# Expert weights in 256-row tiles with two rows to a partition, and later modulation blocks, in a two-layer mixture-of-experts kernel

## The chip, the cores and the metric

The kernel runs on one core of a Trainium2 chip. The metric is the device time of one launch in microseconds (us); less is better. Engines are named as in the profile: PE (TensorE matmul), PEld (its weight load), DVE (VectorE), ACT (ScalarE), POOL (GpSimd), SP (SyncE, which here only issues DMAs). L12 is line 12 of the kernel.

## The reference

All values are float32. A first block has two layers on 512 tokens `x` and, in layer 0, 256 context tokens `xc` (in layer 1 these only serve as keys and values). A layer is a modulated norm, an input projection, four mixers (short convolution, conformer convolution, windowed attention, global attention), an output projection, and an expert stage:

```python
def layer(x, xc, mods, cmods, ...):
    sh1, sc1, g1, sh2, sc2, g2 = split(mods, 6)
    h = rms_norm(x, n1) * (1 + sc1) + sh1
    parts = split_proj(h @ w_in)
    x_new = x + g1 * (concat([ya, yb, yc, yd]) @ w_out)
    h2 = rms_norm(x_new, n2) * (1 + sc2) + sh2
    x_new = x_new + g2 * expert_choice_ffn(h2, router, w_gate, w_up, w_down)

def expert_choice_ffn(h, router, w_gate, w_up, w_down):
    cap = 2 * t // 16
    aff = softmax(h @ router)
    gates, idx = top_k(swapaxes(aff, 1, 2), cap)
    xs = h[idx]
    y = (silu(xs @ w_gate) * (xs @ w_up)) @ w_down * gates
    return zeros.at[idx].add(y)
```

The modulation is `mods = silu(c) @ ada_w[l] + ada_b[l]`, with `ada_w` of 2 x 1024 x 6144, and the same with `c_ctx` for the context. There are 16 experts a layer with three 1024 x 1024 matrices each; an expert takes 64 tokens of `x` and, in layer 0, 32 of `xc`. A second block (gated delta rule, dilated attention, convolutional feed-forward) follows.

## The kernel before, in words

**Entry (L204 to L274, L340 to L400).** SP issues the loads of small parameter rows (`row_load`, L223 to L231, into `rows`), the tokens (`xin`, L234, and `cin`, L265), and four modulation blocks of layer 0 (`ada_load`, L189 to L198, 2 MB each in four pieces). A block is 512 columns of `ada_w`; the norm before the first projection needs blocks 0 to 3. `ada_gen` (L309 to L332) turns one block into its part of `M[l]`: eight matmuls (L318), a copy, four transposes (L327), a sum. Blocks 0, 2, 1, 3 are done in this order, then `norm1_first` norms eight k tiles (128 of 1024 columns each; L396 to L398), and `dense` runs.

**`dense` (L421 to L484).** For each unit of 128 output columns it loads a 512 KB tile `raw`, splits it into a rounded part `wh` (ACT, L442) and the rest `wl` (POOL, L443), and makes three products a k tile (L473, L475). The two query units of an attention take 64 columns of each of two heads, so they are loaded by two DMAs of 64 columns (`colload2`, L493; for the first, L272), in rows of 256 bytes.

**Experts (`experts`, L1026 on).** The routing takes token sums and logits, writes the normed tokens to DRAM (`hd`, L1132), and finds each expert's tokens by eight rounds of maximum (L1145 to L1149). In layer 0, modulation blocks 8 to 11 of layer 1 are made meanwhile (`ga`, stepped at L1120 and L1150), and two accumulators `sumx` and `sumc` in DRAM are zeroed (L1138). An expert gathers its rows of `hd` (L1209), transposes them and applies shift and scale (`xpose`, L1213 to L1230), and then runs gate (`ax`), up (`ux`) and down (`yx`) products, in the order g(e), d(e-1), u(e). In layer 0 a second set (`ac`, `uc`, `yc`) is for the context rows. Each product has eight units, each of 128 rows of a weight (512 KB). The results of experts 0 to 13 are added to `sumx` and `sumc` in DRAM by POOL's DMA; near the end these are read back (`rb`, L1308), transposed and added (`sums_add`), and the last experts' results are added by a scatter with one-hot matmuls (`scatter_x`, `scatter_c`).

**What sets the order of the loads.** `wload` (L1043 to L1056) issues the units in program order, each into the next of a ring of slots: `rawA` (18 in layer 0, 20 in layer 1), `raw` (5) and `rawB` (2 and 8). A slot is free when its matmuls are done. On SP a scheduler sets the order of the instructions by its own estimates.

Of the kernel before, what the change touches and what calls it, by code (L numbers as in the profile page):

```python
# [134 lines left out]
def main_kernel(ctx, tc, I, out, stop=None, dbg=None, manual=False):  # L135
# [37 lines left out]
    dx = pool(ctx, "dx", space=DRAM).tile([128, 8 * 768], F32)  # L173
# [44 lines left out]
    rows = ent.tile([128, 4, 128], F32)  # L218
    xin = xip.tile([128, 4, 1024], F32)
    cin = xip.tile([128, 2, 1024], F32)  # L220
    ada0 = ent.tile([128, 4, 4, 1024], F32)
# [20 lines left out]
    x_load(1)  # L242
    row_load(G, 0, "qn", I["q_norm_g"], 2, dup=True)
    row_load(G, 0, "kn", I["k_norm_g"], 2, dup=True)
    row_load(G, 0, "cbb", I["conv_b_b"].rearrange("l (h p) -> (l h) p", p=128), 4)
    row_load(G, 0, "lng", I["conv_ln_g"].rearrange("l (h p) -> (l h) p", p=128), 4)
    row_load(G, 0, "lnb", I["conv_ln_b"].rearrange("l (h p) -> (l h) p", p=128), 4)
# [3 lines left out]
    x_load(2)  # L251
    SY.dma_start(sinkb, bass.AP(tensor=I["sink"].tensor, offset=I["sink"].offset, ap=[[0, 128], [1, 8]]))
    row_load(SY, 0, "fg", I["final_g"].rearrange("(k p) -> k p", p=128), 8)
    row_load(SY, 0, "ln1", I["ln1_2"].rearrange("l (k p) -> (l k) p", p=128), 8)
    x_load(3)
# [3 lines left out]
    ada_load(0, 0, ada0[:, 0], hfs=(0, 1))  # L259
    row_load(SY, 3, "cq", I["conv_qkv_2"].rearrange("l t (h p) -> (l t h) p", p=128), 48)  # L260
    row_load(SY, 3, "fc", I["ffn_conv_2"].rearrange("l t (h p) -> (l t h) p", p=128), 66)
    ada_load(0, 0, ada0[:, 0], hfs=(2, 3))
    ada_load(0, 2, ada0[:, 2])
    for t in range(2):
        SY.dma_start(cin[:, t, :], I["ctx"][0, t * 128:(t + 1) * 128, :])  # L265
    ada_load(0, 1, ada0[:, 1])
    pre0 = {}
    pre0[0] = raw_tile().rearrange("p (k c) -> p k c", k=8)
    SY.dma_start(pre0[0], I["w_in"][0, :, 1536:1664].rearrange("(k p) c -> p k c", p=128))
    pre0[1] = raw_tile().rearrange("p (k c) -> p k c", k=8)  # L270
    for h in range(2):
        SY.dma_start(pre0[1][:, :, 64 * h:64 * h + 64],  # L272
                     I["w_in"][0, :, 1280 + 128 * h:1344 + 128 * h].rearrange("(k p) c -> p k c", p=128))
    ada_load(0, 3, ada0[:, 3])  # L274
# [34 lines left out]
    def ada_gen(l, blocks, pl, psp):  # L309
        g, o, n = RO["adab"]  # L310
        for b in blocks:
# [8 lines left out]
            if 3 < b < 11 or (l == 1 and b != 7 and b < 11):  # L320
                ada_load(l, b + 1, hfs=range(4 if l == 1 and b > 7 else 3))
# [10 lines left out]
            yield  # L332

# [7 lines left out]
    if True:  # L341
        with ExitStack() as e0:
# [4 lines left out]
            def rows_to_cols(g, n):  # L347
                p = pse.tile([128, 512], F32, name="rc")
                T.transpose(p[:, :n], rows[0:n, g, :], ident[0:n, 0:n])
                V.tensor_copy(cols[:, g, 0:n], p[:, :n])  # L350
# [6 lines left out]
            for t in range(6):  # L357
# [16 lines left out]
                if t == 1:  # L374
                    rows_to_cols(1, RO["n", 1])
# [1604 lines left out]
```

## Time and profile before

| | |
|---|---|
| Time, median of 3 runs (range) | 2650.71 us (2647.95 to 2651.56) |
| Profiled execution: its own time, its span | 2657.17 us, 2655.0 us |
| Busy in the span: PE, PEld, DVE, ACT, POOL | 93%, 57%, 41%, 33%, 24% |
| Moved by DMA | 584.08 MB, mean 220 GB/s |
| Mean granted TensorE clock, share of full | 0.971 |

PE looks busy all over, but a busy share over the span hides the stages: the two expert stages (about 500 to 1057 us and 1389 to 1868 us) move most of the bytes at 380 to 409 GB/s, while the second block from about 1870 us on moves 32 to 130 GB/s. The four views used below are the windows (busy time of each engine, clock, DMA share and GB/s in a stretch), the chain (the work that ended last at each moment, followed back; in each row start, duration, engine or DMA, tile and line), the timeline of an engine, and the waits.

### The profile page before, as it was taken

What the parts mean: (1) busy time and instruction counts of PE and PEld (TensorE: products, weight loads), DVE (VectorE), ACT (ScalarE), POOL (GpSimd) and SP (SyncE); (2) the same over time, 40 slices, a digit from 0 to 9 for tenths busy, and PEclk for the clock granted to TensorE, in tenths of its full rate; (3) what the DMA queues carried; (4) which work ended last, traced back from release to release, by engine and by line L of the source; (5) the groups of instructions that cost most, each with busy time, mean ns of one, the idle gap of its engine ahead of it and who ended that gap; (6) DMA issues with size and microseconds to landing.
All of it is one profiled execution on the core that took longest, in us unless ns stands there. A gap on an engine that the chain in (4) does not pass through costs nothing.

```text
span 2655.0 us, 41308 instructions
## 1 busy us (share of the span) xinstructions
PE 2476.4 (93%) x16415; PEld 1500.4 (57%) x16415; DVE 1092.9 (41%) x2371; ACT 870.2 (33%) x1769; POOL 637.8 (24%) x552
## 2 busy tenths in 40 slices
PE   7999999699999999899979989898899999999998
PEld 4766777344444333577753322132577787888886
DVE  4488852311111113689641102021665555444411
ACT  4544362211111110464531111110562435443422
POOL 3533112011111100633220000000333233444443
PEclk8999999899999999799989999999899999999999
DMA  8454455999999998222179999999421102333332
GB/s 281 140 165 139 149 177 197 322 383 385 385 386 385 388 394 313 58 59 52 61 289 386 394 398 399 399 404 409 130 67 32 40 25 64 95 96 96 92 96 67
DMA packets 324758, 584.08 MB, mean 220 GB/s; under 512 B 36864, under 2 KB 190007, under 8 KB 323927
## 3 DMA queue, kind: packets, MB, share of 16 engines
q1 hardware_dynamic: 311943, 555.16, 57.7%
q0 software_dynamic: 12480, 26.23, 4.1%
q8 instruction: 129, 2.11, 0.3%
q14 instruction: 62, 0.51, 0.1%
q10 hardware_dynamic: 144, 0.08, 0.0%
HBM read 556.74 MB, written 18.87 MB: 217 GB/s over the span
## 4 chain that ended last, share of the span: by engine, by line
PE 62%; DMA 21%; DVE 9%; issue 3%; POOL 2%; ACT 1%; SPq 1%; ACTq 0%; DVEq 0%; POOLq 0%
PE px L473 21%; DMA rawA<-in_w_gate_dram 4%; DMA rawA<-in_w_down_dram 4%; PE ax L1243 3%; DMA rawA<-in_w_up_dram 3%; PE yx L1243 3%; PE ux L1243 3%; PE g L473 2%; PE s L553 2%; PE y L584 2%; PE px L475 2%; DMA rawB<-in_w_gate_dram 2%; PE pt L565 2%; PE ac L1248 2%; PE pt L473 2%
## 5 line engine op out<-in xcount | busy, mean ns | idle before, releaser
L443 POOL TENSOR_TENSOR wl<-raw,wh 128x512 fp32r<-128x512 f32 (+1 forms) x312 | 408.2, 1311 | 962.0 <-ACT wh L442 768.1
L442 ACT ACTIVATE wh<-raw 128x512 fp32r<-128x512 f32 (+1 forms) x312 | 193.6, 625 | 441.2 <-PE px L473 211.0
L473 PE MATMUL px<-hh,wh 128*128 128x512 f32 x768 | 315.7, 412 | 6.4 <-DVE xT L1401 1.8
L473 PE MATMUL px<-hh,wl 128*128 128x512 f32 x768 | 313.1, 408 | 6.6 <-POOL wl L443 6.6
L473 PE MATMUL px<-hl,wh 128*128 128x512 f32 x768 | 314.6, 410 | 3.8 <-DVE hl L1019 1.9
L1225 ACT ACTIVATE xt<-tr,mod,a 128x64 f32<-128x64 f32 x256 | 86.9, 405 | 295.5 <-PE tr L1221 285.1
L473 PEld LDWEIGHTS px<-hh,wh 128*128 128x128 f32 x768 | 148.7, 194 | 41.2 <-issue 6.1
L473 PEld LDWEIGHTS px<-hh,wl 128*128 128x128 f32 x768 | 148.8, 194 | 39.7 <-POOL wl L443 7.3
L473 PEld LDWEIGHTS px<-hl,wh 128*128 128x128 f32 x768 | 148.7, 194 | 37.5 <-issue 3.8
L1369 DVE SCALAR_TENSOR_TENSOR Yx<-yx,gcol,Yx 64x512 fp32r<-64x512 f32 x36 | 27.0, 750 | 268.7 <-ACT Yx L1368 268.7
L1209 POOL DMA_INDIRECT xg<-hd,gidx x32 | 29.7, 927 | 431.9 <-PE tr L1221 398.3
L785 DVE SCALAR_TENSOR_TENSOR yT<-ub,cols,yT 128x512 f32<-128x512 f32 (+1 forms) x180 | 126.5, 718 | 0.6
L1243 PE MATMUL ax<-rawA,xt 128*32 128x512 f32 x856 | 116.8, 597 | 2.2 <-DMA rawA<-in_w_gate_dram 2.1
L1273 ACT ACTIVATE sa<-ax 128x512 f32<-128x512 f32 x32 | 19.1, 597 | 290.9 <-PE ax L1243 183.1
L1300 POOL DMA_INDIRECT sumx<-ys,place x14 | 22.0, 1571 | 376.5 <-ACT ys L1347 376.5
L1243 PE MATMUL ux<-rawA,xt 128*32 128x512 f32 x800 | 106.1, 594 | 0.1
L1237 PE MATMUL ux<-rawA,xt 128*64 128x512 f32 x328 | 87.3, 611 | 8.1 <-DMA rawA<-in_w_up_dram 8.0
L1237 PE MATMUL yx<-rawA,hT 128*64 128x512 f32 x316 | 81.5, 621 | 11.0 <-DMA rawA<-in_w_down_dram 10.0
L565 PE MATMUL pt<-tab,P 128*128 128x128 f32 x448 | 82.2, 284 | 6.8 <-DVE PT L571 4.3
L1368 ACT ACTIVATE Yx<-yx,gcol 64x512 fp32r<-64x512 f32 x36 | 24.6, 682 | 190.7 <-PE yx L1237 138.4
L1228 DVE TENSOR_SCALAR xt<-tr,a,mod 128x32 f32<-128x32 f32 x128 | 39.0, 310 | 115.0 <-ACT xt L1225 114.5
L1237 PE MATMUL ax<-rawA,xt 128*64 128x512 f32 x316 | 77.7, 612 | 7.6 <-DMA rawA<-in_w_gate_dram 7.2
(593 smaller groups left out, 4895.0 us busy)
## 6 DMA issues: line engine op xcount, KB each, us to landing
rawA<-in_w_gate_dram SPq DMA_DIRECT2D x186, 512.0 KB, 10.4
rawA<-in_w_up_dram SPq DMA_DIRECT2D x182, 512.0 KB, 10.2
rawA<-in_w_down_dram SPq DMA_DIRECT2D x151, 512.0 KB, 10.4
raw<-in_ada_w_dram SPq DMA_DIRECT2D x80, 512.0 KB, 5.7
raw<-in_w_down_dram SPq DMA_DIRECT2D x74, 512.0 KB, 10.2
raw<-in_w_gate_dram SPq DMA_DIRECT2D x62, 512.0 KB, 8.1
raw<-in_w_in_dram SPq DMA_DIRECT2D x56, 512.0 KB, 3.9
raw<-in_w_up_dram SPq DMA_DIRECT2D x55, 512.0 KB, 10.2
```

Of the source, the lines that this page charges most:

```text
L442: A.activation(wh[:, :n], raw[i][:, a:a + n], AF.Copy)
L443: G.tensor_tensor(wl[:, :n], raw[i][:, a:a + n], wh[:, :n].bitcast(F32), op=OP.subtract)
L473: T.matmul(px, lhsT=w[:, k % 4, :], rhs=h[:, k0 + k, 0:512], start=st, stop=sp_)
L475: T.matmul(pc, lhsT=w[:, k % 4, :], rhs=h[:, k0 + k, 512:nt], start=st, stop=sp_)
L553: T.matmul(s[:, :w], lhsT=q, rhs=k, start=(a == 0), stop=(a == len(mm) - 1))
L565: T.transpose(pt[:, (t - a) * 128:(t - a + 1) * 128], P[:, t * 128:(t + 1) * 128], ident)
L584: T.matmul(y[64 * g:64 * g + 64, bi * 128:(bi + 1) * 128], lhsT=vs[g][t], rhs=PTs[i, g][t // 4][:, (t % 4) * 128:(t % 4 + 1) * 128], start ...
L785: V.scalar_tensor_tensor(acc[:, j, o:o + n], src, w, acc[:, j, o:o + n], op0=OP.mult, op1=OP.add)
L1225: A.activation(xt[:, kk, 0:64], p[:, k * NX:k * NX + 64], AF.Identity, bias=M[l][:, 24 + kk, 0:1], scale=a2[:, kk, 0:1])
L1237: T.matmul(px[64 * g:64 * g + 64, :], lhsT=lx(u), rhs=w[:, 512 * hf:512 * hf + 512], start=first, stop=last)
L1243: T.matmul(px[32 * g:32 * g + 32, :], lhsT=lx(u)[:, 32 * (g % 2):32 * (g % 2) + 32], rhs=w[:, 512 * hf:512 * hf + 512], start=first, stop= ...
L1248: T.matmul(pc[32 * g:32 * g + 32, :], lhsT=lc(u), rhs=w[:, 256 * q:256 * q + 256], start=first, stop=last)
```

## The change

1. Expert weights come in tiles of 256 rows, `[128, 2, 1024]`: partition p holds rows 2p and 2p+1, one run of 8 KB, by one load of 1 MB (9 slots of `rawA` and 1 of `rawB` in layer 0, 10 and 4 in layer 1; together with 2 pairs of `raw` 12 and 16 slots). The pairs of `raw` are two loads of 512 KB, each with runs of 4 KB. A load is issued at every second unit. The rows of a matrix are so taken in another order; `hd` is written with its columns in the matching order, shift and scale are permuted once (`shsc`), and activation and product write the hidden values in that order.
2. In the loop over the experts SP keeps the program's order.
3. Blocks 8 to 11 of layer 1's modulation are loaded behind all of layer 0's expert weights, into slots of `rawA`, and made between the steps of the last scatter.
4. At the entry, tokens and blocks 0 and 2 come first, then `cin`, the first unit, blocks 1 and 3, the two query units as one pair of 256-column loads (1 KB runs; also at the later query units), and then most of the small rows. The first norm is made in two halves, tiles 0 to 3 after blocks 0 and 2, tiles 4 to 7 after 1 and 3, with `dense` started between.
5. `sumx` and `sumc` are zeroed in the output projection's stage, and read back and added one expert sooner.

```diff
+    for t in range(1, 4):
+        x_load(t)
+    ada_load(0, 0, ada0[0])
+    ada_load(0, 2, ada0[2])
...
+    SY.dma_start(pre0[0], I["w_in"][0, :, 1536:1664].rearrange("(k p) c -> p k c", p=128))
+    ada_load(0, 1, ada0[1])
+    ada_load(0, 3, ada0[3])
+
+    def pair_load(src, c0):
+
+        ts = [raw_tile(), raw_tile()]
+        for i, t in enumerate(ts):
+            SY.dma_start(t.rearrange("p (k c) -> p k c", k=4),
+                         src[512 * i:512 * i + 512, c0:c0 + 256].rearrange("(k p) c -> p k c", p=128))
+        return ts
+
+    pre0[1] = pre0[2] = pair_load(I["w_in"][0], 1280)
...
+                    norm1_first(range(4), a1)
+                    gd = dense(units, hh, hl, dw, psp, pre=pre0, ahead=4)
+                    next(gd)
+                    drain(ada_gen(0, (1, 3), sqp, psp))
+                    norm1_first(range(4, 8), a1)
...
+                    G.memset(lg[:, 0:512], 0.0)
+                    for acc_, n in zip(accs, (8, 4)):
+                        SY.dma_start(acc_.rearrange("(p a) c -> p (a c)", p=128).rearrange("p (b c) -> p b c", c=512),
+                                     lg[:, None, 0:512].to_broadcast([128, n, 512]))
...
-            units = [(w, e, u) for w, e in seq for u in range(8)]
+            units = [(w, e, u) for w, e in seq for u in range(4)]
+            if has:
+
+                units += [("ada", b, u) for b in range(8, 12) for u in range(2)]
...
-            slots = ["A"] * nA + ["W"] * 5 + ["B"] * nB
+            slots = ["A"] * (nA // 2) + ["W"] * 2 + ["B"] * (nB // 2)
...
+                    src = W[w][l, e, 256 * u:256 * u + 256, :].rearrange("(p i) c -> p i c", i=2)
                     if k == "W":
-                        r = raw_tile()
-                    elif k == "A":
-                        r = rwpA.tile([128, 1024], F32, name="rawA", bufs=nA)
+                        r = [raw_tile(), raw_tile()]
+                        for j in range(2):
+                            SY.dma_start(r[j], src[:, j, :])
                     else:
-                        r = rwpB[0].tile([128, 1024], F32, name="rawB", bufs=nB)
-                    SY.dma_start(r, W[w][l, e, 128 * u:128 * u + 128, :])
-                    wt[w, e, u] = r
+                        if k == "A":
+                            t = rwpA.tile([128, 2, 1024], F32, name="rawA", bufs=nA // 2)
+                        else:
+                            t = rwpB[0].tile([128, 2, 1024], F32, name="rawB", bufs=nB // 2)
+                        SY.dma_start(t, src)
+                        r = [t[:, 0, :], t[:, 1, :]]
+                    for j in range(2):
+                        wt[w, e, 2 * u + j] = r[j]
...
-                    ga = ada_gen(1, range(8, 12), mp, Psum(ps, {"yx": 1}, {"misc": "yx"})) if has else iter(())
...
-                    for _ in steps(ga, 2):
-                        pass
-                    wload(6 if l else 0)
+                    wload(3 if l else 0)
...
-                        if i in (2, 4, 6):
-                            for _ in steps(ga, 2):
-                                pass
...
-                        wload(1)
+                        wload(u % 2)
...
                         if last and has:
+                            next(ga)
                             sq_add(sp, stA[:, 0:512], xT[:, m, :], 512, m == 0, eng=G)
...
+                with tc.manual_schedule(engines={mybir.EngineType.SP}):
+                    gather(0)
+                    gather(1)
+                    xpose(0)
...
+                            if has and e in (12, 14):
+                                for t in ((4, 5), range(4))[e // 2 - 6]:
+                                    sums_load(t)
```

The order of SP's loads at the entry, before (`ada_89` holds all four modulation blocks, in four calls of L196 in the order 0, 2, 1, 3; `raw` of L269 and L272 are the first two units):

```order
L196 DMA ada_89<-in_ada_w_dram 128x2x512 x6
L265 DMA cin<-in_ctx_dram 128x1024 x2
L196 DMA ada_89<-in_ada_w_dram 128x2x512 x4
L269 DMA raw<-in_w_in_dram 128x8x128
L272 DMA raw<-in_w_in_dram 128x8x64 x2
L196 DMA ada_89<-in_ada_w_dram 128x2x512 x4
L621 DMA dx<-xT 128x4096
```

and now (`ada_96`, `ada_97`, `ada_94`, `ada_95` are blocks 0, 2, 1, 3; L232 and L234 are the small rows):

```order
L239 DMA xin<-in_x_dram 128x1024 x3
L199 DMA ada_96<-in_ada_w_dram 128x2x512 x4
L199 DMA ada_97<-in_ada_w_dram 128x2x512 x4
L252 DMA cin<-in_ctx_dram 128x1024 x2
L254 DMA raw<-in_w_in_dram 128x8x128
L199 DMA ada_94<-in_ada_w_dram 128x2x512 x4
L199 DMA ada_95<-in_ada_w_dram 128x2x512 x4
L262 DMA raw<-in_w_in_dram 128x4x256 x2
L232 DMA raw<-in_q_norm_g_dram 2x64 x2
```

The last two blocks moved ahead of the query loads, and the small rows behind these.

PE in layer 0's routing, before, from the end of the top-k on (`tg` and `ti` are its results, `xg` the gathered rows of expert 0, L318 and L327 the modulation's matmuls and transposes):

```order
L1161 MATMUL tr<-tab,tg 128x80
L1162 MATMUL tr<-tab,ti 128x80
L318 MATMUL yx<-raw,s_74 32x512 x4
L1221 MATMUL tr<-tab,xg 128x96 x5
L318 MATMUL yx<-raw,s_74 32x512 x2
L1221 MATMUL tr<-tab,xg 128x96 x3
L1243 MATMUL ax<-rawA,xt 32x512 x4
L1248 MATMUL ac<-rawA,xt 32x256 x4
L1243 MATMUL ax<-rawA,xt 32x512
L318 MATMUL yx<-raw,s_74 32x512 x2
```

and now:

```order
L1205 MATMUL tr<-tab,tg 128x80
L1206 MATMUL tr<-tab,ti 128x80
L1265 MATMUL tr<-tab,xg 128x96 x8
L1287 MATMUL ax<-rawA,xt 32x512 x4
L1292 MATMUL ac<-rawA,xt 32x256 x4
```

No modulation matmul stands between the top-k and the experts any more. They stand on PE in the tail of layer 0 now, between the last `yc`, the scatter (L1448 for `x`, L1476 for the context) and layer 1's sums (L310):

```order
L1292 MATMUL yc<-rawB,hT 32x256 x4
L1367 MATMUL tr<-tab,rb 128x128 x4
L326 MATMUL ux<-rawA,s_76 32x512 x5
L1448 MATMUL tr<-oh,Yx 128x512
L326 MATMUL ux<-rawA,s_76 32x512 x3
L1448 MATMUL tr<-oh,Yx 128x512 x3
L335 MATMUL ux<-tab,ys 128x128 x4
L1448 MATMUL tr<-oh,Yx 128x512 x4
L326 MATMUL ux<-rawA,s_76 32x512 x6
```

The first block's matmuls moved ahead of the scatter's first; the other three follow among its later ones. On SP their loads stand behind the last weights and ahead of layer 1's first projection:

```order
L1092 DMA raw<-in_w_down_dram 128x1024 x4
L1098 DMA rawB<-in_w_down_dram 128x2048
L1081 DMA rawA<-in_ada_w_dram 128x2x512 x16
L500 DMA raw<-in_w_in_dram 128x8x128
L262 DMA raw<-in_w_in_dram 128x4x256 x2
```

They moved behind every expert load of layer 0.

## Rows read from the trace of the kernel before

**Rows 1.** Windows: us, busy (count) of PE PEld DVE ACT POOL, PEclk, DMA share, GB/s.

```profile
0.00:50.00 50.00, 33.25 (x140) 14.69 (x141) 13.32 (x42) 22.43 (x44) 8.63 (x15) 0.90 0.93 315
...
450.00:500.00 50.00, 30.11 (x180) 16.91 (x179) 25.11 (x107) 13.01 (x20) 4.52 (x28) 0.81 0.70 249
...
550.00:850.00 300.00, 300.00 (x3642) 124.40 (x3638) 45.15 (x118) 40.07 (x100) 37.66 (x28) 1.00 1.04 386
...
850.00:1050.00 200.00, 196.22 (x2220) 74.75 (x2210) 42.10 (x112) 28.65 (x68) 17.81 (x17) 1.00 1.02 380
...
1050.00:1100.00 50.00, 39.25 (x172) 24.81 (x173) 39.45 (x83) 25.02 (x47) 16.44 (x14) 0.73 0.12 38
...
1400.00:1850.00 450.00, 406.80 (x1730) 120.32 (x1726) 70.28 (x104) 67.36 (x165) 11.54 (x13) 1.00 1.03 399
...
1900.00:2655.00 755.00, 734.96 (x3740) 589.82 (x3738) 351.52 (x623) 314.90 (x551) 294.45 (x230) 1.00 0.24 70
```

**Rows 2.** Chain of waits, 0 to 110 us: start, us, what.

```profile
24.78 5.11 SPq L272
...
29.93 4.29 SPq L272
...
36.24 6.55 DMA ada<-in_ada_w_dram
...
49.39 0.55 DVE xin L397
...
63.97 1.11 POOL hl L398
```

**Rows 3.** Chain of waits, 430 to 530 us.

```profile
463.40 3.60 DMA raw<-in_ada_w_dram
...
480.82 15.39 DMA raw<-in_ada_w_dram
...
504.64 6.05 DMA raw<-in_ada_w_dram
...
520.29 0.43 PE ux L1243 x4
...
525.01 0.81 PE tr L1221 x8
```

**Rows 4.** Chain of waits, 1340 to 1400 us.

```profile
1380.17 0.49 DVE idx L1147 x2
...
1384.05 4.07 DMA xg<-hd,gidx
...
1389.46 8.34 PE ax L1237 x32
```

**Rows 5.** Timeline of PE, 700 to 716 us: start, us, instructions.

```profile
702.57 1.04 PE L1243 MATMUL ax<-rawA,xt 128*32 128x512 f32 x8
...
703.86 1.04 PE L1243 MATMUL ax<-rawA,xt 128*32 128x512 f32 x8
```

**Rows 6.** Chain of waits, 1000 to 1130 us.

```profile
1044.30 7.13 DMA rb<-sumx
...
1057.29 0.69 ACT Yx L1368
```

**Rows 7.** Timeline of PE, 451 to 530 and 1050 to 1100 us.

```profile
464.97 0.66 PE L327 MATMUL yx<-tab,sq 128*128 128x128 f32 x4 [0.74 <-ACT sq L323]
...
465.91 2.19 PE L318 MATMUL yx<-raw,s 128*32 128x512 f32 x8 [0.28 <-DVE mod L329]
...
1083.39 0.80 PE L473 MATMUL px<-hh,wh 128*128 128x512 f32 x1 [1.17 <-ACT hh L416]
```

**Rows 8.** Windows of layer 1's experts and of the load of xT.

```profile
379.00:380.00 1.00, 1.00 (x12) 1.00 (x10) 1.00 (x4) 0.81 (x2) 1.00 (x2) 1.00 1.02 418
...
380.00:381.00 1.00, 1.00 (x9) 0.80 (x8) 1.00 (x2) 0.00 (x0) 1.00 (x1) 1.00 0.95 393
...
1820.00:1840.00 20.00, 20.00 (x87) 6.91 (x83) 7.11 (x10) 0.60 (x1) 0.00 (x0) 1.00 1.03 410
```

More of the change, by code (lines that the diff above doesn't have):

```diff
@@ L332, in ada_gen, with rows_to_cols @@
             yield
+    def rows_to_cols(psp, name, g, n):
+        p = psp.tile([128, 512], F32, name=name)
+        T.transpose(p[:, :n], rows[0:n, g, :], ident[0:n, 0:n])
+        V.tensor_copy(cols[:, g, 0:n], p[:, :n])
     es_l0 = ExitStack()
@@ L379, in main_kernel, with norm1_first @@
             drain(ga)
-            for g in (0, 2, 3):
-                rows_to_cols(g, RO["n", g])
-            V.tensor_scalar(nsink, sinkb, -1.0, None, op0=OP.mult)
-        entry.close()
-        def norm1_first(sqp):
-            a1 = sqp.tile([128, 8, 2], F32, name="a1")
-            for k in range(8):
+        entry2.close()
+        def norm1_first(ks, a1):
+            for k in ks:
                 if k % 4 == 0:
@@ L429, in load @@
                     raw[i] = pre[i]
+                elif i < len(units) and len(units[i]) == 6 and units[i][5]:
+                    raw[i] = raw[i - 1]
+                elif i < len(units) and len(units[i]) == 6:
+                    raw[i] = units[i][0]()
                 elif i < len(units):
@@ L615, in layer @@
                 psp = Psum(ps, {"px": 3, "s": 2, "pt": 1, "misc": 1, "y": 1}, {"pc": "px"})
+                c0 = dict(a_b=0, a_c=256, a_h=512, b_v=768, b_g=1024, c_q=1280, c_k=1536, c_v=1664,
+                          d_q=1792, d_k=2048, d_v=2176)
+                evs = []
+                units = []
+                for n in "c_k c_q c_v b_g b_v d_k d_q d_v a_c a_h a_b".split():
+                    for j in range(2 if n[2] == "q" or n[0] in "ab" else 1):
+                        nt, ev = NT if n[2] == "q" or n[0] in "ab" else 768, partial(lambda i, px, pc: evs[i](px, pc), len(units))
+                        if n[2] == "q":
+                            units.append((partial(pair_load, w_in, c0[n]), ev, nt, 0, 8, j))
+                        else:
+                            units.append((colload(w_in, c0[n] + 128 * j), ev, nt))
                 if has:
                     hh, hl = hh0, hl0
-                    norm1_first(sqp)
+                    a1 = cst.tile([128, 8, 2], F32)
+                    norm1_first(range(4), a1)
[3 more added lines that the diff above has]
+                    norm1_first(range(4, 8), a1)
+                    entry.close()
                     xip_es.close()
@@ L938, in layer @@
                     ga = ada_rest()
-                gd = dense(u_c + u_b + u_d + u_a, hh, hl, dw, psp, pre=pre0 if has else {}, ahead=4 if has else None)
+                else:
+                    ga = iter(())
+                if not has:
+                    gd = dense(units, hh, hl, dw, psp)
                 at, cv = att_gen(), conv31()
                 w1, w2, w3 = (28, 28, 64) if has else (18, 18, 44)
-                run_all((dense_part(gd, 12), 12))
+                if has:
+                    for _ in range(2):
+                        next(gd)
+                    for g in (0, 2, 3):
+                        rows_to_cols(psp, "misc", g, RO["n", g])
+                    V.tensor_scalar(nsink, sinkb, -1.0, None, op0=OP.mult)
+                run_all((dense_part(gd, 9 if has else 12), 12))
                 run_all((dense_part(gd, 12), 12), (steps(at, w1), w1), (steps(ga, 8), 8))
@@ L1080, in experts @@
                 gidx = mp.tile([128, 16], I32)
+                shsc = mp.tile([128, 2, 8, 2], F32)
                 iota = mp.tile([128, 512], F32)
```

203 lines of the change are left out of this document (97 added, 106 removed).

## The prediction

> **What bounds the kernel now.** I read the table of windows first, to see which engine is full in which stage, then the chain of waits at each place where PE is not full. The reader should find four kinds of stage in [rows 1]. (a) The entry, 0 to 50 us: PE 33.25 of 50 us, DMA share 0.93 at 315 GB/s. (b) The routing of layer 0, 450 to 500: PE 30.11 of 50, clock 0.81. (c) The experts of layer 0, where both PE (300 of 300, then 196.22 of 200) and DMA (share 1.02 to 1.04, 380 to 386 GB/s) are full. (d) The experts of layer 1, 1400 to 1850: DMA share 1.03 at 399 GB/s with PE busy 406.80 of 450, so DMA sets the pace. The last 755 us are PE's (734.96 busy); the change does not touch them. All times below are from one execution of 2657.17 us (span 2655.0), 6.5 us above the median of 2650.71; I subtract the sum from the median.
>
> **A. Entry (+12 us).** In the chain, two q loads hold SP's queue for 5.11 and 4.29 us [rows 2]: 1024 rows of 256 B each. Behind them the last modulation block (in_ada) is issued and lands at 36.24 + 6.55 = 42.8. The norm begins at 49.4 and its eight k tiles end with hl at 65.1, 15.7 us or about 2 us a tile. The change puts the two q loads, as 256-column pieces with 1 KB rows, and all but four small row loads behind the blocks: block 3 then lands 9.4 us sooner, at about 33.4. Blocks 0 and 2 go first and let tiles 0 to 3 be normed before block 3 is there, so that only four tiles (7.9 us) remain after it. 33.4 + 6.6 (landing to first tile now) + 7.9 = 48, against 65.1: 17 us. The bounds are 5 (the dense steps that follow are held by POOL's and ACT's splitting of the weights, which does not get faster) and 17. I take 12, nearer the upper one, since the queue hold alone is 9.4. The remaining small loads then stand ahead of the next w_in load, some 18 issues on SP; the first three units are loaded by then, which covers them.
>
> **B. Routing of layer 0 (+23).** PE takes instructions in order, and modulation blocks 8 to 11 of layer 1 stand among the routing's. Three waits on their loads are on the chain: 3.60 us ahead of the top-k's input D, 15.39 after the top-k (where the transposes of the gathered rows stand behind), and 6.05 inside the first expert [rows 3]. The first up matmuls (ux) begin at 520.3. The top-k has ended where the second wait begins, 480.8; without the blocks it ends 3.6 sooner, at 477.2. Layer 1 shows the rest without such blocks: from the end of the last index (1380.7), over a gather of 4.07, to the first matmul (1389.5) it takes 8.8 us [rows 4]. So 486.0, plus eight units of 1.29 [rows 5] and one set of transposes (0.81, [rows 3]): ux at 497.1, 23 sooner. Bounds: 15, if the gather or the copies of ht are then late, and 25, the sum of the three waits. Added here are eight tiny matmuls and two DVE copies for the permuted shift and scale; they hide behind the top-k, which runs 12 us on DVE, and cost under 1 us if not. The zeroing of the accumulators (3 MB written, 8 us at 386 GB/s) goes ahead of the routing; behind it on SP stand weights first used after 486, which cover it.
>
> **C. Experts of layer 0 (+13).** From 550 to 850 PE gets 3642 instructions through in 300 us, 12.14 a us; from 850 to 1050 it is 2220 in 200, 11.10 a us [rows 1]. At the first rate those would take 183 us: 17 us are lost there, to weights that come too late once the lead of the first 25 tiles is eaten, and to the sums (rb waits 7.13 at the end, [rows 6]). After the change the lead at ux is larger (no block loads amid the weights) and rb is loaded one expert sooner. An expert is 24 units of 512 KB and two sets of transposes, 24 x 1.29 + 1.6 = 32.6 us on PE, 1.36 a unit. DMA brings 12.6 MB of weights and some 0.8 MB of gathered and added rows an expert (96 rows of 4 KB each way): 13.4 MB at 386 GB/s is 34.7 us, 1.44 a unit. With 8 KB runs in ten slots of twelve (E) I expect 1.41. Over the 15 experts that follow, that is a lag of 0.05 x 360 = 18 us, some 13 units: the lead at ux (24 loaded before the first expert, 8 used, some 5 brought back: about 21) lasts; at 1.44 it would be 29 us, 20 units, which leaves nothing for delays. Bounds 5 and 17; I take 13.
>
> **D. Tail of layer 0 (-7).** The blocks now come last in the weight stream and their matmuls stand between the scatter's on PE. One block is 2.19 us of matmuls and 0.66 of transposes [rows 7], four are 11.4. Between 1050 and 1100 PE is idle 10.8 of 50 us [rows 1]; I put 4.4 of the 11.4 into such gaps. Their 8 MB land about 22 us after the last weight at 386 GB/s, but that weight should land some 8 us ahead of PE's last use, and the last block is needed some 14 us after it: just in time. Bounds -2 (all hidden) and -15 (the loads late by 8). Layer 1's first w_in loads stand behind the blocks on SP; their tiles are first used at 1083.4 now [rows 7], 26 us after the last expert, and would land some 16 us after it (24 behind the last weight), so they are covered by about 10.
>
> **E. Experts of layer 1 (+10).** Here a faster load is a faster kernel. Weights in 4 KB runs alone make 410 GB/s at share 1.03; the one load with 8 KB runs in this trace, xT<-dx, makes 418 at share 1.02 in one full microsecond and 393 at 0.95 in the next [rows 8]. Brought to one share both are 3 to 4% more than 410; as they stand, 2% more and 4% less. 512 KB at 410 GB/s is 1.279 us; 3% is 0.038 a unit. 352 units are still to be loaded when this stage begins, 14 slots in 16 get long runs: 308 x 0.038 = 12 us. Against it, one slot less (1.3 us) and two units instead of one behind the last load (0.9). I take +10. Bounds: 393 GB/s gives 1.334 a unit, 308 x 0.055 = 17 us lost; 4% and no loss gives 16 won. The nearest row is the microsecond with the full share. [...]
>
> **F.** The second block's first weights are issued in program order instead of waiting for the last matmul: +1. ACT's and DVE's strided activation and product are used a pass later, ten us of cover.
>
> Sum: 12 + 23 + 13 - 7 + 10 + 1 = 52, so 2650.7 - 52 = **2598.7, say 2598.5 us**.
>
> **Rivals.** *Long runs are no faster* (chance 0.17): 8 KB behaves as 4 KB. For it: 393 in one of the two rows. Against: 418 in the other. E becomes -2 and C falls to 8, since the lead ends before the stream: 35 us, 2616. [...] *The blocks stall the tail* (0.12): the weights land no sooner than PE's last use, and PE waits behind 22 us of block loads with only 7 us of it covered, so D is -22: 2614. For it: DMA is full to the end of layer 0. *The entry's gain is not kept, or the change does not do what it says there* (0.10): the dense steps after it go by the splitting of weights, A is 5, or SP's order puts the row loads in the way: 2606. *Slower* (0.06): 8 KB runs are slower under load, for instance because gathered rows wait behind packets that are twice as long. With runs of 8 KB as fast as now the gain is the first rival's 35 us. Each 512 KB that takes d longer than 1.279 is lost 308 times in layer 1 and, the lead being gone, some 300 times in layer 0, so the point from which it decides is d = 35/608 = 0.058 us, 392 GB/s. At 10% less than 410, 369 GB/s (d = 0.142), it is 35 - 86 = -51: 2702. The 393 row is at this point, the 418 row speaks against it.
>
> **How the numbers follow.** My forecast has 0.55. The rivals but the last lie at 2606 to 2616. With the upper ends of A, B and E together it would be near 2580, and two of the milder rivals together near 2625: the range is 2578 to 2626, leaving about 0.1 above and 0.1 below. This kernel's measurement can tell about 0.2%, 5 us. Faster: 0.55 + 0.17 + 0.12 + 0.10 less a little for several mishaps at once, 0.91. Within 0.2%: 0.03, at 390 to 394 GB/s or with several losses at once. Slower: 0.06.
>
> **What would show it.** A: the first px at or before 45 and the last hl near 50, no wait of SP at the q loads. B: no PE wait on in_ada between 455 and 500 of the old scale, ux near 485 once A is taken off. C: PE's rate over 12 instructions a us until the last expert. D: the stretch from the last yc to the first px of layer 1 some 7 us longer than 26. E: 415 to 425 GB/s in stretches of layer 1 without gathers. I am wrong if these stretches show 410 or less, if PE waits on in_ada after the last expert for over 10 us, or if what the entry gains is gone by 100 us.

## The result, and the profile after

The changed kernel takes 2616.74 us (median of 4 runs, 2612.24 to 2619.82), the kernel before, on the same chips, 2651.14 (2647.95 to 2656.49). The ratio is 0.9867 with a 95% interval of 0.9844 to 0.9890: 34 us faster, where 52 were forecast (2598.5); the time lies inside the range that was given, near the first two rivals' 2614 to 2616. The profiled execution of the changed kernel took 2619.82 us, its span is 2618.1; against the profile of before that is 36.9 us of span.

Where these came from is read by cutting both spans at the same events of the trace: the copy of layer 0's logits (`lg`), the first up matmul (`ux`), the last down matmul (`yx`), layer 1's first projection matmul (`px`), its logits, its first gate matmul (`ax`), its last `yx`.

| Stage, us | before | after | gained | forecast |
|---|---|---|---|---|
| start to layer 0's logits | 458.2 | 448.9 | 9.3 | A 12 |
| to the first ux | 60.6 | 43.3 | 17.3 | B 23 |
| to the last yx of layer 0 | 538.4 | 530.7 | 7.7 | C 13 |
| to layer 1's first px | 26.2 | 31.5 | -5.3 | D -7 |
| to layer 1's logits | 279.1 | 275.7 | 3.4 | 0 |
| to its first ax | 27.0 | 28.2 | -1.2 | 0 |
| to its last yx | 478.7 | 473.6 | 5.1 | E 10 |
| the rest | 786.8 | 786.2 | 0.6 | F 1 |

The windows of the changed kernel (columns as in [rows 1]):

```profile
0.00:50.00 50.00, 35.77 (x178) 20.08 (x179) 21.74 (x54) 29.33 (x56) 11.79 (x14) 0.97 0.86 296
450.00:500.00 50.00, 35.97 (x321) 19.48 (x325) 25.95 (x112) 16.84 (x33) 3.71 (x4) 0.80 0.55 208
550.00:850.00 300.00, 300.00 (x3642) 124.46 (x3638) 44.58 (x117) 39.25 (x99) 36.59 (x27) 1.00 1.03 391
850.00:1000.00 150.00, 146.19 (x1695) 59.64 (x1691) 32.33 (x89) 23.73 (x56) 14.23 (x13) 1.00 1.02 400
1400.00:1800.00 400.00, 347.77 (x1516) 114.33 (x1516) 65.17 (x97) 58.38 (x143) 9.77 (x11) 0.99 1.02 406
1760.00:1810.00 50.00, 43.62 (x192) 14.15 (x189) 9.81 (x14) 5.03 (x12) 0.00 (x0) 1.00 1.01 418
```

Against [rows 1] and [rows 8] the reader sees the rate of DMA in layer 1's experts go from 399 to 406 GB/s, without gathers from 410 to 418, and in layer 0's from 386 to 391; PE still falls from 3642 instructions in 300 us to 1695 in 150, 11.3 a us, in the late experts of layer 0. The chain at the entry:

```profile
38.67 0.50 PE px L486
...
47.33 0.55 DVE xin L401
...
51.93 1.14 POOL hl L402
```

The tiles that came from 49.39 to 63.97 in [rows 2] have matmuls behind them from 38.67 on, and the last but one hl begins at 51.93. The chain in layer 0's routing:

```profile
448.93 0.69 DVE lg L999
...
468.94 0.49 DVE idx L1194 x2
...
473.46 4.29 DMA xg<-hd,gidx
...
479.40 1.87 PE ax L1287 x8
...
482.12 1.71 PE ax L1287 x8
...
484.61 0.86 PE ax L1287 x8
...
492.35 0.86 PE ux L1287 x8
```

Against [rows 3] no modulation load is left between the logits and ux. The gather is followed at once by the first gate matmuls, whose first two units take 1.87 and 1.71 us against 0.86 for the third: PE has just waited 7.3 us for the gather, and the granted clock is 0.50 until 484.4 and 1.00 from 484.6 on:

```profile
479.00:483.80 4.80, 4.80 (x31) 1.50 (x33) 2.44 (x8) 2.75 (x8) 0.90 (x1) 0.50 0.32 85
484.60:492.30 7.70, 7.70 (x103) 2.91 (x96) 0.00 (x0) 0.27 (x1) 0.00 (x0) 1.00 0.85 322
```

In the tail the blocks' matmuls (L326) stand among the scatter's (timeline of PE):

```profile
1023.81 1.91 PE L326 MATMUL ux<-rawA,s 128*32 128x512 f32 x10
...
1054.41 0.80 PE L486 MATMUL px<-hh,wh 128*128 128x512 f32 x1 [1.17 <-ACT hh L420]
```

and at the end of layer 1's experts (chain) the last load, now of 1 MB, is followed by two units of PE:

```profile
1814.81 15.09 DMA rawB<-in_w_down_dram
...
1829.94 1.96 PE yx L1281 x8
```

### The profile page after: what moved, and what is told of

It is laid out like the page before. It is cut to its first block, busy times and chain, and to the rows that moved or that the text cites. A ratio compares the mean times of both kernels' runs of the same rounds, so it can differ in the third digit from the quotient of the medians.

```text
span 2618.1 us, 40657 instructions
## 1 busy us (share of the span) xinstructions
PE 2440.2 (93%) x16447; PEld 1505.9 (58%) x16447; DVE 1096.5 (42%) x2375; ACT 869.1 (33%) x1769; POOL 630.8 (24%) x545
## 4 chain that ended last, share of the span: by engine, by line
PE 63%; DMA 22%; DVE 9%; POOL 2%; issue 2%; ACT 2%; SPq 0%; ACTq 0%; DVEq 0%; POOLq 0%
PE px L486 21%; DMA rawA<-in_w_down_dram 7%; DMA rawA<-in_w_gate_dram 4%; DMA rawA<-in_w_up_dram 3%; PE yx L1287 3%; PE ax L1287 3%; PE ux L1287 3%; PE g L486 2%; PE y L591 2%; PE s L560 2%; PE px L488 2%; PE pt L572 2%; PE pt L486 2%; PE s L486 2%; PE yc L1292 2%
## 5 line engine op out<-in xcount | busy, mean ns | idle before, releaser
L1269 ACT ACTIVATE xt<-tr,shsc 128x64 f32<-128x64 f32 x256 | 86.2, 405 | 280.8 <-PE tr L1265 273.8
L1287 PE MATMUL ux<-rawA,xt 128*32 128x512 f32 x1024 | 133.9, 594 | 0.0
L1287 PE MATMUL yx<-rawA,hT 128*32 128x512 f32 x976 | 127.6, 594 | 4.2 <-DMA rawA<-in_w_down_dram 3.6
L1281 PE MATMUL yx<-rawA,hT 128*64 128x512 f32 x288 | 70.7, 625 | 21.2 <-DMA rawA<-in_w_down_dram 21.2
L1272 DVE TENSOR_SCALAR xt<-tr,shsc 128x32 f32<-128x32 f32 x128 | 38.9, 310 | 117.8 <-ACT xt L1269 117.1
L1281 PE MATMUL ux<-rawA,xt 128*64 128x512 f32 x320 | 78.9, 601 | 9.2 <-DMA rawA<-in_w_up_dram 9.2
L1281 PE MATMUL ax<-rawA,xt 128*64 128x512 f32 x352 | 83.5, 609 | 1.9 <-DMA rawA<-in_w_gate_dram 1.8
```

The source lines that it names most:

```text
L1269: A.activation(xt[:, kk, 0:64], p[:, k * NX:k * NX + 64], AF.Identity, bias=shsc[:, 0, kk, 0:1], scale=shsc[:, 1, kk, 0:1])
L1281: T.matmul(px[64 * g:64 * g + 64, :], lhsT=lx(u), rhs=w[:, 512 * hf:512 * hf + 512], start=first, stop=last)
L1287: T.matmul(px[32 * g:32 * g + 32, :], lhsT=lx(u)[:, 32 * (g % 2):32 * (g % 2) + 32], rhs=w[:, 512 * hf:512 * hf + 512], start=first, stop= ...
```

## The experiments

Each is one edit to the changed kernel unless it says otherwise. Times are medians, ratios to the kernel before on the same chip, with 95% intervals; stage times are read as in the table above, from one profiled execution each.

**1. Short runs again.** Every 1 MB load becomes two of 512 KB with runs of 4 KB.

```diff
-                        SY.dma_start(t, src)
+                        for j in range(2):
+                            SY.dma_start(t[:, j, :], src[:, j, :])
```

> The changed kernel with each 1 MB weight load cut into two loads of 512 KB, one for each row of a partition, so that every run is 4 KB again; slots, order and all else stay. Theory (the length of the run is what the two expert stages gained by): layer 1's experts, from first gate matmul to last down matmul, go from 473.6 us back to about 479 to 481, stretches without gathers from 419 GB/s to 410, and layer 0's experts end 3 to 6 us later; in all 8 to 12 us slower than the changed kernel, about 2627. Rival (order and size of the loads, not the run): layer 1's experts stay at 473 to 475 and the time within 3 us of 2617.

Measured: 2633.23 us, ratio 0.9912 (0.9889 to 0.9934): slower than the changed kernel by 12 us going by the ratios, 16 by the medians. Layer 1's experts take 480.6 us (473.6 with long runs), layer 0's 538.6 (530.7). The windows:

```profile
550.00:850.00 300.00, 299.26 (x3630) 123.76 (x3622) 44.66 (x117) 39.33 (x99) 36.63 (x27) 1.00 1.03 385
850.00:1000.00 150.00, 144.56 (x1620) 55.16 (x1616) 29.84 (x83) 21.28 (x52) 14.24 (x13) 1.00 1.03 391
1400.00:1800.00 400.00, 357.80 (x1500) 103.44 (x1497) 60.82 (x90) 60.19 (x149) 10.37 (x12) 1.00 1.03 399
1760.00:1810.00 50.00, 45.98 (x194) 13.35 (x192) 11.13 (x16) 5.91 (x13) 0.00 (x0) 1.00 1.03 409
```

The rates are within 1% of those of before, 385, 391, 399 and 409 GB/s against 386, 387 (from 850 to 1000), 399 and 410, where long runs make 391, 400, 406, 418. The run length is worth 7.9 us in layer 0 and 7.0 in layer 1. The theory holds, a little above its upper bound in layer 0; and without long runs the paired tiles are 2 us behind the kernel before in layer 1 (480.6 against 478.7), which the forecast had as 2.2.

**2. Long runs, half the partitions a load.** To tell the run from the size of a load.

```diff
-                        SY.dma_start(t, src)
+                        for j in range(2):
+                            SY.dma_start(t[64 * j:64 * j + 64], src[64 * j:64 * j + 64])
```

> The changed kernel with each 1 MB load cut into two loads of 512 KB by partitions (0 to 63, 64 to 127), so that runs stay 8 KB and loads are as small as before. Theory (run length): as the changed kernel, layer 1's experts 473 to 475 us, about 2617, or up to 3 us better in layer 0, since a unit is held up by 512 KB and not by 1 MB. Rival (the size of a load): layer 1's experts near 479, about 2625.

Measured: 3279.68 us, ratio 1.2333 (1.2274 to 1.2393). Neither held; the windows in layer 1's experts say why:

```profile
1800.00:1850.00 50.00, 33.06 (x104) 9.95 (x104) 2.88 (x4) 4.44 (x11) 0.89 (x1) 0.75 1.02 233
1950.00:2000.00 50.00, 29.90 (x98) 8.65 (x100) 2.88 (x4) 4.44 (x11) 0.89 (x1) 0.79 1.02 227
```

DMA is busy all the time (share 1.02) and moves 227 to 233 GB/s: little over half of the changed kernel's 406 to 418 in this stage, at the same share (1.01 to 1.02). Runs are as long as there and loads as small as before, where the stage made 399 to 410; what neither kernel has is a load that covers 64 partitions in a row.

**3. Long runs, every second partition a load.** The same sizes and the same runs, but each load covers every second one of the 128 partitions.

```diff
-                        SY.dma_start(t, src)
+                        for j in range(2):
+                            SY.dma_start(t[j::2], src[j::2])
```

> The changed kernel with each 1 MB load cut into two of 512 KB by even and odd partitions, runs of 8 KB. With the lower and upper 64 partitions DMA fell to about 230 GB/s. Theory (half of the partitions in a row share half of the way into SBUF, and every second one does not): over 400 GB/s again, layer 1's experts 473 to 480 us, about 2617 to 2622; then run length alone, at the old load size, carries the gain. Rival (a load that covers 64 partitions is slow whichever they are): about 230 GB/s and 3250 us again.

Measured: 2643.82 us, ratio 0.9949 (0.9929 to 0.9969); layer 1's experts 475.9 us, layer 0's 548.6. The windows:

```profile
550.00:850.00 300.00, 290.83 (x3526) 121.46 (x3522) 44.63 (x117) 39.31 (x99) 36.64 (x27) 1.00 1.03 389
850.00:1000.00 150.00, 136.89 (x1603) 57.60 (x1596) 28.80 (x82) 18.58 (x44) 13.81 (x13) 0.97 1.00 386
1400.00:1800.00 400.00, 347.81 (x1542) 121.47 (x1538) 59.60 (x88) 61.10 (x152) 10.65 (x12) 0.97 1.02 405
1760.00:1810.00 50.00, 44.31 (x188) 14.47 (x184) 6.54 (x9) 8.12 (x20) 0.00 (x0) 0.91 1.01 418
```

The rate is back at 405 and 418 GB/s, as the theory had it, so what slowed experiment 2 was which partitions a load covers (of the way into SBUF the runs show these rates alone), and in layer 1 a load of 512 KB with long runs is within 2.3 us of one of 1 MB: there the run's length carries the gain. In layer 0 the time was missed: from 550 to 850 PE already loses (3526 instructions against 3642) at 389 GB/s, where the changed kernel has 391. The weights are not the reason. The waits of PE over this run's layer 0 experts (485 to 1034; us in total, times, longest) hold none for a weight:

```profile
PE tr L1368 <- DMA rb<-sumx: 7.2, 1, 7.2
PE tr L1266 <- DVE hT L1342: 6.8, 12, 0.6
PE tr L1341 <- DVE sa L1334: 6.7, 15, 0.5
```

In the changed kernel PE has no such wait before 850. Its transposes of `sa` stand among the gate units there, and those of the gathered rows among the up units. Here the scheduler has put both between the up units and the next gate units, where they wait for DVE, 13.5 us in all; a sum (`rb`) costs 7.2 more. It is 33.87 us from one expert's first gate matmul to the next's, 32.85 in the changed kernel. So in layer 0 the edit also changed PE's order, and the run says nothing there on the size of a load.

**4. The kernel before without blocks 8 to 11.**

```diff
-                    ga = ada_gen(1, range(8, 12), mp, Psum(ps, {"yx": 1}, {"misc": "yx"})) if has else iter(())
+                    ga = iter(())
...
-            if has:
-                ada_load(1, 8)
...
+    V.memset(M[1][:, 32:48, :], 0.0)
```

> The kernel before without modulation blocks 8 to 11 of layer 1: their loads and matmuls are left out and that part of the modulation is zero, so 8 MB and 11 us of PE are gone. Theory (the blocks' loads held layer 0's routing): the first up matmuls of layer 0 begin 18 to 24 us sooner than 518.8, at 495 to 501, and the experts end 18 to 28 sooner; about 2625 to 2632. Rival (the first expert was waiting for its weights or for the gather anyway): under 10 us, 2642 or more.

Measured: 2630.26 us, ratio 0.9911 (0.9894 to 0.9927). From the logits to ux it takes 43.8 us (60.6 before, 43.3 after): the waits were the blocks' and nothing else's. The first ux comes 24.8 us sooner (494.1 against 518.8), but 7.9 of them lie ahead of the logits (450.3 against 458.2), a stretch that varies by as much (last section). Its timeline of PE, two gate units and the first of ux:

```profile
482.46 1.94 PE L1242 MATMUL ax<-rawA,xt 128*32 128x512 f32 x8
...
485.02 1.04 PE L1242 MATMUL ax<-rawA,xt 128*32 128x512 f32 x8
...
494.06 1.03 PE L1242 MATMUL ux<-rawA,xt 128*32 128x512 f32 x8
```

Layer 0's experts then take 531.6 us, with 4 KB runs and single tiles: 6.8 less than in the kernel before, since the blocks' loads no longer stand amid the weights, and nearly the changed kernel's 530.7. These 6.8 and the 16.8 up to ux make the whole 24 us of the ratio. Beside experiment 1 (538.6, 4 KB runs, paired tiles, SP in program order) this puts the price of pairing, one slot of 25 less and a slot pair that frees only after two units, at some 7 us in layer 0: the long runs first had to pay for it. This is read from two runs; pairing alone was not undone, and program order may be up to 2 of the 7 (experiment 11).

**5. The changed kernel without blocks 8 to 11.**

```diff
-                units += [("ada", b, u) for b in range(8, 12) for u in range(2)]
+                pass
...
-                    ga = ada_gen(1, range(8, 12), Psum(sp, {"ys": None}, {"sq": "ys"}), Psum(ps, {"ux": 1}, {"misc": "ux"}))
+                    ga = iter(range(99))
...
+    V.memset(M[1][:, 32:48, :], 0.0)
```

> The changed kernel without modulation blocks 8 to 11 of layer 1: their loads and matmuls are left out and that part of the modulation is zero. Theory (in the tail the blocks cost PE time between the scatter's matmuls, 5 to 6 us): from the last yc matmul of layer 0 to the first px of layer 1 it takes 25 to 27 us instead of 31, about 2611. Rival 1 (they are hidden): within 2 us of 2617. Rival 2 (their 8 MB also hold back the rows read back for the sums or layer 1's first weights): over 9 us, 2607 or less.

Measured: 2610.82 us, ratio 0.9830 (0.9813 to 0.9846); the tail takes 26.1 us, layer 0's experts 531.5.

Its timeline of PE, from the last transpose of the sums to layer 1's first px:

```profile
1024.74 0.66 PE L1368 MATMUL tr<-tab,rb 128*128 128x128 f32 x4
...
1031.72 4.60 PE L1449 MATMUL tr<-oh,Yx 128*128 128x512 f32 x8 [0.49 <-DVE xT L1452]
...
1050.53 0.79 PE L487 MATMUL px<-hh,wh 128*128 128x512 f32 x1 [1.17 <-ACT hh L421]
```

The theory holds: 5.4 us in the tail (31.5 against 26.1) and nothing in the stage ahead of it, so the 8 MB behind the weights hold back nothing there. PE is the price, not the loads. The whole is 10 us by the ratios, of which the stages show these 5.4 alone; the two intervals touch, so the whole cannot tell 5 from 10. The windows of the two tails, first the changed kernel's, show why 80 matmuls more cost only this:

```profile
1023.00:1054.00 31.00, 26.59 (x142) 11.84 (x134) 22.15 (x49) 17.07 (x33) 15.22 (x13) 0.95 0.53 170
```

```profile
1024.80:1050.50 25.70, 17.38 (x56) 11.29 (x54) 19.81 (x42) 15.03 (x30) 12.77 (x11) 0.62 0.05 13
```

PE is 9.2 us longer busy and 3.9 less idle, and with the blocks among the scatter's matmuls the granted clock is 0.95 instead of 0.62; the scatter's own 32 matmuls take 9.7 us in all instead of 12.8 (sums over the timelines). In the tails of nine kernels with the blocks there (the changed one, experiments 1, 3 and 7 to 12) it is 0.94 to 0.99, in four without (the kernel before, experiments 4, 5 and 6) 0.56 to 0.73.

**6. The blocks in layer 1's body.** Loaded and made there between its projection and attention steps; their loads and steps in layer 0's tail are left out as in experiment 5.

```diff
-                    ga = iter(())
+                    ga = ada_gen(1, range(8, 12), sqp, psp)
```

> The changed kernel with modulation blocks 8 to 11 of layer 1 made among layer 1's projection and attention steps, where DMA has a share of 0.23, instead of in layer 0's tail. The tail is 5.4 us shorter without them. Theory 1 (PE has gaps in layer 1's body which they fill): the stretch from layer 1's first px to its logits grows by 2 to 6 us from 275.7, in all 0 to 4 us faster than the changed kernel. Theory 2 (PE is full there): it grows by the blocks' 11 us, in all 5 us slower.

Measured: 2628.35 us, ratio 0.9898 (0.9881 to 0.9914). The tail gets its 5.4 us back (26.1), layer 1's body goes from 275.7 to 293.5. Its window of that body, and then the changed kernel's:

```profile
1042.00:1335.00 293.00, 272.77 (x1534) 200.76 (x1534) 206.60 (x442) 145.53 (x314) 104.04 (x88) 0.97 0.37 119
```

```profile
1054.00:1330.00 276.00, 256.87 (x1454) 198.57 (x1454) 202.01 (x435) 143.64 (x312) 103.38 (x88) 0.96 0.30 96
```

PE is busy 15.9 us longer: theory 2, with a size above its 11 (the body varies by some 6 us between kernels without blocks there, see below). The whole is 8 us slower than the changed kernel by the ratios. The tail is the cheaper place.

**7. The first norm in one piece.**

```diff
-                    norm1_first(range(4), a1)
+                    drain(ada_gen(0, (1, 3), sqp, psp))
+                    norm1_first(range(8), a1)
                     gd = dense(units, hh, hl, dw, psp, pre=pre0, ahead=4)
                     next(gd)
-                    drain(ada_gen(0, (1, 3), sqp, psp))
-                    norm1_first(range(4, 8), a1)
```

> The changed kernel with the first norm made in one piece again: all eight k tiles after all four modulation blocks, then the dense steps; the order of the loads stays as changed. Theory (the split norm is worth about four tiles of 2 us, the order of the loads the rest of the 10 to 11 us that the last hl gained): the last hl at 60 to 63 us instead of 54.9, the logits of layer 0 5 to 8 us later, about 2622 to 2625. Rival (the dense steps behind are paced by POOL's splitting, so the half norm is given back): the last hl later, but the logits of layer 0 within 2 us of 448.9 and the time within 3 us of 2617.

Measured: 2619.52 us, ratio 0.9862 (0.9845 to 0.9878), the same as the changed kernel. The first px starts at 34.2 us (34.1 with the split), and the last hl in POOL's timeline stands at

```profile
53.26 1.10 POOL L402 TENSOR_TENSOR hl<-cin,hh 128x256 fp32r<-128x256 f32 x1 [0.23 <-DVE cin L401]
```

so the last hl did not move (54.4 against 54.9). Neither the theory nor the rival: the first px at 34.2, and the fourth hl of POOL at 36.3 in both kernels, show that the scheduler puts the first four tiles ahead by itself. The split in the program's text is worth nothing; what it is worth that four tiles go ahead, this run cannot tell, since they still do.

**8. The query loads ahead of blocks 1 and 3 again,** in their new form.

```diff
-    ada_load(0, 1, ada0[1])
-    ada_load(0, 3, ada0[3])
...
     pre0[1] = pre0[2] = pair_load(I["w_in"][0], 1280)
+    ada_load(0, 1, ada0[1])
+    ada_load(0, 3, ada0[3])
```

> The changed kernel with the two query units' 256-column loads (1 KB runs) put ahead of modulation blocks 1 and 3 again, where the two 64-column loads (256 B runs) stood before. Theory (the form of the loads is what held SP for 9.4 us; their place matters by their transfer alone): the last hl about 3 us later than the 54 to 56 us of the changed kernel and its variants, of the 10 us that the entry gained. Rival (the place is what counts): the last hl 7 us or more later, near 62.

Measured: 2620.22 us, ratio 0.9880 (0.9857 to 0.9902); the last hl ends at 55.4. Place costs 0.5 us, less than the theory's 3, and the rival falls. SP's timeline:

```profile
15.73 5.70 SPq L260 DMA_DIRECT2D raw<-in_w_in_dram  x2
21.47 9.25 SPq L199 DMA_DIRECT2D ada<-in_ada_w_dram  x8
```

The two loads of 1 KB rows hold SP for 5.7 us, against 9.4 for the old ones [rows 2]. The first of them takes 4.61 of the 5.7; in the changed kernel, where a modulation load is issued at that moment (16.46), that load holds SP for 4.61 too, so this part is not the form's.

**9. The small rows on POOL.** The 15 calls behind the query loads, and the sink, issued by POOL at the start.

```diff
-    row_load(SY, 0, "qn", I["q_norm_g"], 2, dup=True)
+    row_load(G, 0, "qn", I["q_norm_g"], 2, dup=True)
...
```

> The changed kernel with the small row loads that stand behind the two query units on SP (15 calls and the sink) issued by POOL at the start instead, so that the load of the fourth projection unit, issued at 44.9 us, goes out at about 32. Theory (they hold SP in front of weights that are then late; part of the entry's gain is lost there): the logits of layer 0 2 to 4 us sooner than 448.9 us, outside the 3 to 5 us by which this stretch differs between executions only if they are all of that. Rival (covered, as forecast): no difference in the time, within 3 us of 2617.

Measured: 2623.87 us, ratio 0.9884 (0.9865 to 0.9904). The fourth unit's load goes out at 34.5 us (SP's timeline),

```profile
34.51 2.59 SPq L500 DMA_DIRECT2D raw<-in_w_in_dram  x1
```

ten sooner, and the logits come at 448.6 (448.9): covered, as forecast. The time is, if anything, longer.

**10. The sums read back late again.**

```diff
-                            if has and e in (12, 14):
-                                for t in ((4, 5), range(4))[e // 2 - 6]:
+                            if has and e in (13, 14):
+                                for t in ((4, 5), range(4))[e - 13]:
...
-                            elif has and e == 14:
-                                run_gu("u", e, mid, lambda u: sums_add(8 + u // 2))
```

> The changed kernel with the sums read back and added as before (read after experts 13 and 14, added in the up and down products of expert 15). Theory (at the end of layer 0 the sums, read 11 us before they are used behind a full DMA queue, cost a wait that the change took away): layer 0's experts 4 to 7 us longer than 530.7 us, about 2621 to 2624. Rival (the wait was the weights', and the time is the same whichever comes last): within 2 us in the stage, and within 3 us of 2617.

Measured: 2618.14 us, ratio 0.9858 (0.9838 to 0.9879); layer 0's experts 530.4 us. PE now does wait for a sum again (its timeline),

```profile
1013.40 0.63 PE L1367 MATMUL tr<-tab,rb 128*128 128x128 f32 x4 [1.60 <-DMA rb<-sumx]
```

but what it waits there it would wait for weights: the rival.

**11 and 12. Without program order on SP,** alone and with experiment 9's rows.

```diff
-                with tc.manual_schedule(engines={mybir.EngineType.SP}):
+                with nullcontext():
```

> The changed kernel with SP's order left to the scheduler in the loop over the experts too. Theory (program order gives at most the 1 us ahead of the second block): within 3 us of 2617. Rival (the scheduler's estimates put loads behind waits, and program order carries part of what the expert stages gained): over 5 us slower, with longer expert stages than 530.7 and 473.6 us.

> Both of the last candidates for a better kernel together: the small row loads on POOL, and SP's order in the expert loop left to the scheduler (which alone measured 0.9853 of the kernel before against 0.9867 for the changed kernel, the intervals overlapping). Theory (the expert stages gain 2 us each without the program order): 0.984 to 0.985 of the kernel before, 2 to 6 us faster than the changed kernel. Rival (the two are the same kernel in time): 0.986 to 0.988.

Measured: 2614.37 us, ratio 0.9853 (0.9832 to 0.9875), and 2618.26, ratio 0.9860 (0.9843 to 0.9878). The expert stages are 528.6 and 471.6, then 527.2 and 473.3 us. Experiment 11's theory and experiment 12's rival hold. Program order carries nothing, and if anything the stages are some 2 us shorter without it; both are the changed kernel in time, and no kernel of this study that computes everything is clearly faster than it.

## Why the prediction was right, point by point

The sign and the places were right; 52 us were reckoned where 34 came, the gains A, B, C and E being each too large by 3 to 6 us.

**A, 12 forecast, 9.3 measured.** The last hl came 10.2 us sooner (65.1 to 54.9). The traces divide this the other way round from the prediction. The step that failed is "block 3 then lands 9.4 us sooner". The last piece of block 3 is issued 9.8 us sooner (27.0 against 36.8), in part since the first block goes out 5.1 us sooner, with small rows behind it (timelines of SP, before and after):

```profile
9.42 0.91 SPq L196 DMA_DIRECT2D ada<-in_ada_w_dram  x2
```

```profile
4.30 6.75 SPq L199 DMA_DIRECT2D ada<-in_ada_w_dram  x8
```

But the block's last matmuls end only 2.7 us sooner, at 43.5 against 46.2 (timelines of PE, before and after):

```profile
42.84 3.35 PE L318 MATMUL misc<-ada,s 128*32 128x512 f32 x8 [0.40 <-DMA ada<-in_ada_w_dram]
```

```profile
42.40 1.07 PE L326 MATMUL misc<-ada,s 128*32 128x512 f32 x8
```

When block 3 landed after the change, the trace does not tell; PE stands in the products of `dense` from 38.67 to 42.40. The step "so that only four tiles (7.9 us) remain after it" held. In the changed kernel POOL makes four hl by 37.4 and the other four from 48.3 on, where all eight stood from 50.4 to 65.1 (timeline of POOL, after):

```profile
36.27 1.12 POOL L402 TENSOR_TENSOR hl<-cin,hh 128x256 fp32r<-128x256 f32 x1 [0.23 <-DVE cin L401]
...
48.32 1.12 POOL L402 TENSOR_TENSOR hl<-cin,hh 128x256 fp32r<-128x256 f32 x1 [2.30 <-DVE cin L401]
```

So 2.1 of the 10.2 us are the earlier start of the tiles behind block 3, and 8.1 that four remain instead of eight. What in the change lets four go ahead stays open: neither the split in the program's text (experiment 7) nor the place of the query loads (experiment 8) does. That 12 came near owes something to luck: the sum gave 17, with 9.4 us of which 2.1 came, and was cut to 12 by choice.

**B, 23 forecast, 17.3 measured; shown by experiment 4.** The step that failed is the copy of layer 1's rest onto layer 0. With "without the blocks it ends 3.6 sooner" it reckoned 19.0 us from the logits to the end of the last index; it is 20.5 now (448.93 to 469.43). From there to the first ax it is 10.0 against layer 1's 8.8 [rows 4]. The eight units then take 12.9 us, not 11.1, although no transposes are among them: the first two run at a granted clock of 0.50, which costs the 2.6 us over 8 x 1.29. The other 1.5 is the start of ux, which I took from the chain (520.3) where the timeline has 518.8.

**C, 13 forecast, 7.7 measured.** The reading of the cause held in part: from one expert's first gate matmul to the next's PE takes 32.85 us until the lead is gone, in both kernels, and then goes at DMA's pace. "With 8 KB runs in ten slots of twelve (E) I expect 1.41" failed, and with it that the lead lasts: DMA's rate rose from 386 to 391 GB/s, 1.3%, where 2 were reckoned, and PE still falls to 11.3 instructions a us after 850. The larger lead that C named is worth 6.8 us (experiment 4) and the long runs 7.9 (experiment 1); the sums' earlier place gave nothing (experiment 10). Paired tiles and program order take some 7 back (experiments 1 and 4), and this is a term that C, unlike E, put at nothing. Each of these is a difference of two single executions. "17 us are lost there" counted losses that stayed.

**D, -7 forecast, -5.3 measured.** Shown by experiment 5, with the right cause, PE's time and not the loads. The row of 2.19 us that was taken for a block's matmuls holds 8 of its 16; the 16 of a block take 1.93 (timeline of PE before),

```profile
462.30 1.93 PE L318 MATMUL yx<-raw,s 128*32 128x512 f32 x16
```

so four blocks are 10.4 and not 11.4 us. PE's busy time grew by 9.2, at the higher clock of experiment 5, which the sum did not have, and 3.9 went into gaps, near the 4.4 that were put there.

**E, 10 forecast, 5.1 measured; the term was mis-sized.** The cause, run length, is shown by experiment 1, the price of pairing (2.2) by the same run (1.9). The step that failed is "Brought to one share both are 3 to 4% more": the plain 2% of the row at 418 was right. Without gathers it is 418 against 409 to 410, inside the 415 to 425 that was named as the sign, and with them 406 against 399, 1.8%. These rates hold long and short runs together, so they go with all 352 units: 352 x 1.279 x 0.018 = 8.1 us, where experiment 1 measured 7.0 and the sum had 12. The measured 1.8 to 2.2% stand against the 3% of the sum.

**The stages called 0.** Layer 1's body gained 3.4 us, with later query loads in 1 KB rows, but it varied from 275.7 to 281.7 us among the kernels that have this change and no block there: no cause is shown.

**The rivals.** "Long runs are no faster" had the right time, 2616, for a wrong reason. "The blocks stall the tail" (2614) is out by experiment 5, and the slower side by the rates of experiment 1. "The entry's gain is not kept" put A at 5; 9.3 us of it are there at layer 0's logits, in a stretch that varies by 8.

## What to carry to other kernels

A load that cannot be hidden is worth the length of its runs: 8 KB against 4 KB gave 1.8% under gathers and 2.2% without in layer 1, and paired tiles cost part of it back in ring slots. Modulation matmuls that stand among the routing's cost PE the whole wait for their loads, 17 us, though only layer 1 needs them: move the wait first, and price what is left by the engine's own time, and its clock, in the place it goes to. When only a load was edited, PE's order can still have changed (experiment 3): read the waits before the cause is named. A tile that is loaded in halves is not cut at partition 64: so cut, layer 1's weights came at 227 to 233 GB/s, by every second partition at 405 to 418 (experiments 2 and 3).

## What the runs showed that was not expected

In layer 1's experts loads to 64 partitions in a row ran at 227 to 233 GB/s, to every second partition at 405 to 418 with the same bytes and runs. With the blocks among the scatter's matmuls the granted clock of layer 0's tail is 0.94 to 0.99, without them 0.56 to 0.73 (experiment 5), and the blocks' 10.4 us of PE cost 5.4. And the clock fell where PE did not idle: in the kernel before, window 350 to 400,

```profile
350.00:400.00 50.00, 50.00 (x327) 38.92 (x326) 28.83 (x67) 28.14 (x51) 7.83 (x6) 0.93 0.61 207
```

PE is busy all 50 us at a mean clock of 0.93. From 382 to 388 it is 0.50; just before, PE ran 32 matmuls of 16 columns (the last 20 in its timeline):

```profile
380.61 3.51 PE L1009 MATMUL misc<-rw,mod 128*128 128x16 f32 x20
```

In experiment 4, whose program has the same matmuls, the clock is 1.00 from 350 to 400. From the last hl to layer 0's logits, kernels with the same code took from 387.8 to 396.0 us, which is as much as most parts of this change are worth: a part's price is to be read from its own stage, not from the whole.
